# A two-layer decoder trunk on one NeuronCore: the compressed attention branch turned three steps later, one projection step ahead of the first scores, and two start-up jobs on other engines

## The chip, the cores and the metric

The kernel runs on one NeuronCore of a Trainium2 chip, in one launch. Its time is the device time of one execution in microseconds (us). The engines are TensorE (PE in the profile; PEld is its weight load), VectorE (DVE), ScalarE (ACT), GpSimd (POOL) and SyncE (SP), each with its own in-order instruction queue. They wait for each other through semaphores. DMA transfers are issued from an engine's queue and move their data beside it.

## The reference

The trunk has a width of 1024 and 512 positions. Layer 0 mixes with an RG-LRU and a retention head group, layer 1 with a native sparse attention (NSA). Each layer has an FFN behind it. What the change touches is the first projection of layer 0 and the attention of layer 1:

```
def reference(x, ...):
    h = x
    for layer in range(2):
        hn = rmsnorm(h, attn_norm[layer])
        h = h + (hybrid_ab(hn, ...) if layer == 0 else nsa(hn, ...))
        h = h + swiglu(rmsnorm(h, ffn_norm[layer]), ...)
    return rmsnorm(h, final_norm)

def nsa(h, w_in, ..., w_out):              # 16 heads in 4 groups, head size 64
    proj = h @ w_in                        # queries, six K/V sets, gates
    ...
    s = einsum('bqgrd,bngd->bgrqn', qb, kc)         # compressed branch: 31 blocks
    p_cmp = where(vis, softmax(where(vis, s, NEG)), 0)
    o_cmp = einsum('bgrqn,bngd->bqgrd', p_cmp, vc)
    ...                                             # selected and window branches
    o = gb[..., 0:1] * o_cmp + gb[..., 1:2] * o_slc + gb[..., 2:3] * o_win
    return o @ w_out
```

## The kernel before

All products are made in a split form. An operand is kept as a rounded part and a remainder (`whi` and `wlo` for weights, `hgh` and `hgl` for activations, `oh` and `ol` for the attention's output), and three matmuls take the place of one (`mm3`, lines 201 to 203). ACT makes the rounded part by a copy, DVE the remainder by a subtraction. A scheduler takes the program's instructions with priorities and fixes the order on each engine when the kernel is built; at run time every engine then works strictly in that order.

**Start (`layer0`, lines 449 to 478).** PE first runs 20 small matmuls on zeros (`ps_z`, line 373). Then the first projection runs over k = 0..7. Slice k needs a weight slice (`wr`, DMA line 462) and an input slice (`xin`, DMA line 463), 256 KB each, both on SP's queue. ACT rounds the weights (line 464), ACT and DVE make `hgh` (line 234) and `hgl` (line 235) from the input, DVE makes `wlo` (line 466), and PE runs 12 matmuls per k into `ps_x` (lines 476 to 478), in the order of k, since they accumulate.

**Attention (`attention`, from line 1092).** Positions are cut in four tiles of 128, taken in the order 2, 3, 1, 0; a unit is a tile, one of four groups g and its branches. A unit's scores (`head_s`, lines 1174 to 1176), the scaling of its probabilities on POOL (`scale`, line 1194), and their transposes and products with V (lines 1199, 1203, 1206, 1214, 1215) stand three units apart, and the loop runs in slots, four or more to a unit. At a slot's end two things may be advanced by one step:

- `fill`: what is left of layer 1's projection, 20 steps of 6 matmuls (`ps_t`).
- `side`: a list of generators, advanced once a slot (twice if it is longer than 2). One is `compressed(i)` for tile i: scores, maximum, subtraction on POOL, exponential on ACT, sum on DVE, then the multiplication by the gated reciprocal on POOL (line 1136, out and in `pcmp`), some empty steps, four PE transposes (line 1142), the rounded part `pch` on ACT (line 1144) and the remainder `pcl` on DVE (line 1145). Another is `finish`, which carries an output out (`up` line 1226, `o` line 1231, `oh` line 1235, `ol` line 1237).

The last matmuls of an output (`block_v`, lines 1220 and 1221) take `pch` and `pcl` of its tile. The transposes of the compressed branch and those of line 1199 share a pool of two buffers (`ps_tr`), each of which is free when ACT and DVE have read it.

**Output projection (`layer1`).** Behind the last unit, 72 matmuls into `ps_p` (4 output tiles, 6 of 8 slices k, three each) begin before the last outputs are there; slices 0 and 1 come from tile 0's group 0, 2 and 3 from group 1, and so on. Its weights `w1o` are loaded by SP into the buffers (`wr`) that the attention's probabilities use, so that a load waits until a unit's transposes are done, and are then rounded on ACT (line 136) and DVE (line 137).

Of the kernel before, what the change touches and what calls it, by code (L numbers as in the profile page):

```python
# [63 lines left out]
class Trunk:  # L64
# [377 lines left out]
    def layer0(self):  # L442
        nc, a = self.nc, self.a
# [13 lines left out]
        for k in range(KD):  # L457
            x = xin[k // 4][:, k % 4, :]
            c = slice((k % 4) * S, (k % 4 + 1) * S)
            w = raws[k // 4][:, c]  # L460
            hi, lo = (t[:, (k % 2) * S:(k % 2 + 1) * S] for t in wx[k // 2])
            nc.sync.dma_start(w, a["w0t"][k // 4][:, c])
            nc.sync.dma_start(x, a["xT"][k])
            nc.scalar.copy(hi, w)
            self.put_hg(hg, k, x, self.gain[0][:, k:k + 1])
            nc.vector.tensor_tensor(lo, w, hi.bitcast(F32), op=ALU.subtract)
        for k in range(KD):
# [113 lines left out]
        w = [self.unit() for _ in range(4)]  # L581
# [510 lines left out]
    def attention(self, QS, stack, stacked, qlate, halves, KH, KL, VV, kc2, vc, gate, OH, OL, fill):  # L1092


        nc = self.nc
# [4 lines left out]
        def compressed(i):  # L1100

            while not {(i, 0), (i, 1)} <= stacked:
                yield
            q = QS[i]
            pc = self.g2([P, H, 32], name="pcmp")
            pr = pc.rearrange("p (r g) n -> p r g n", g=G)
            mask = self.cmask[:, i:i + 1, :].unsqueeze(1).broadcast_to([P, R, 2, 32])
            for half in range(2):
                ps = self.psA("ps_s")
                ph = ps.rearrange("p (r g z n) -> p r g z n", r=R, g=2, z=2)  # L1110
                for h in range(8 * half, 8 * half + 8):
                    g, r = h // R, h % R
                    T.matmul(ph[:, r, g % 2], q[:, h, :], kc2[:, g], start=True, stop=True)
                    if h % 4 == 3:
                        yield
                dst = pr[:, :, 2 * half:2 * half + 2, :]
                V.tensor_tensor(dst, ph[:, :, :, 0, :], mask, op=ALU.add)
                V.tensor_tensor(dst, ph[:, :, :, 1, :], dst, op=ALU.add)
                yield
            mx = self.s1([P, H], "mx")  # L1120
            V.tensor_reduce(mx, pc, axis=AX.X, op=ALU.max)
            yield
            Q.tensor_tensor(pc, pc, mx.unsqueeze(2).broadcast_to([P, H, 32]), op=ALU.subtract)
            yield
            A.activation(pc, pc, AF.Exp)
            yield
            sc = self.s1([P, H], "sc")
            V.tensor_reduce(sc, pc, axis=AX.X, op=ALU.add)
            V.reciprocal(sc, sc)
            gv = gate[:, i, :].rearrange("p (g r b) -> p b r g", g=G, r=R)  # L1130
            s3 = sc.rearrange("p (r g) -> p r g", r=R)
            V.tensor_tensor(s3, s3, gv[:, 0], op=ALU.mult)
            if i == 0:
                V.tensor_scalar(sc, sc, self.vis0, None, op0=ALU.mult)
            yield
            Q.tensor_tensor(pc, pc, sc.unsqueeze(2).broadcast_to([P, H, 32]), op=ALU.mult)
            yield
            yield
            pt = self.psC("ps_tr")
            pcf = pc.rearrange("p h n -> p (h n)")  # L1140
            for r in range(R):
                T.transpose(pt[:, r * P:(r + 1) * P], pcf[:, r * P:(r + 1) * P], self.ident)
            ch, cl = (self.g2([P, S], F32R, name="pc" + n) for n in "hl")
            A.copy(ch, pt)
            V.tensor_tensor(cl, pt, ch.bitcast(F32), op=ALU.subtract)
            cmp_pt[i] = ch, cl
            yield

        def late(t):
            QS[t] = self.b8([P, H, P], F32R, name="qs")  # L1150
            for c in range(2):
                stack(t, qlate[:, halves[1].index(t), 8 * c:8 * c + 8, :].rearrange("p h d -> p (h d)"), c)
                yield
# [11 lines left out]
        def head_s(u, r):  # L1165
            if r == 0:
                u.p = self.probs().rearrange("p (r b x) -> p r b x", r=R, b=u.n)
                u.rs = self.sm.tile([P, R, u.n], F32, tag="rs", name="rs")
                u.kh, u.kl = (x[u.g // 2][:, u.bs[0]:u.bs[-1] + 1, u.g % 2, 0:u.nk] for x in (KH, KL))
            h = R * u.g + r  # L1170
            ps = self.psA("ps_s")
            u.ps = ps[:, 0:u.n * u.nk].rearrange("p (b x) -> p b x", b=u.n)
            q = QS[u.i][:, h, :]
            T.matmul(u.ps, q, u.kh, start=True, stop=False)
            T.matmul(u.ps, q, u.kl, start=False, stop=False)
            T.matmul(u.ps[:, :, u.i * P:u.nk], self.identr, self.triNeg.unsqueeze(1).broadcast_to([P, u.n, P]), start=False, stop=True)

        def head_m(u, r):
            u.nm = self.sm.tile([P, 2], F32, tag="nm", name="nm")
            V.tensor_reduce(u.nm[:, 0:u.n], u.ps, axis=AX.X, op=ALU.max, negate=True)  # L1180

        def head_e(u, r):
            for b in range(u.n):
                A.activation(u.p[:, r, b, 0:u.nk], u.ps[:, b, :], AF.Exp, bias=u.nm[:, b:b + 1], accum_out=u.rs[:, r, b:b + 1])  # L1184
# [11 lines left out]
        def block_t(u, b, j):  # L1196
            u.pt = self.psC("ps_tr")
            for r in range(R):
                T.transpose(u.pt[:, r * P:(r + 1) * P], u.p[:, r, b, j * P:(j + 1) * P], self.ident)
            u.th, u.tl = (self.g2([P, S], F32R, name="pt" + n) for n in "hl")  # L1200

        def block_hi(u, b, j):
            A.copy(u.th, u.pt)

        def block_lo(u, b, j):
            V.tensor_tensor(u.tl, u.pt, u.th.bitcast(F32), op=ALU.subtract)
            u.last = u.th, u.tl
# [36 lines left out]
        def advance():  # L1244
            if side and next(side[0], 0) == 0:
                side.pop(0)
                advance()
# [4 lines left out]
        for n in range(len(units) + LAG):  # L1252
            us = units[n] if n < len(units) else None
            if n >= len(units):

                self.plan("w1o", n - len(units), 2048)
                self.load()
                self.prefetch(2)
            un = units[n - 1] if 0 <= n - 1 < len(units) else None
            uv = units[n - LAG] if n >= LAG else None  # L1260
            if us is not None and us.g == us.bs[0] == 0:
                at = tiles.index(us.i)
                if at + 1 < NT:
                    t = tiles[at + 1]
                    side += ([late(t)] if t in halves[1] else []) + [compressed(t)]
            nb = len(uv.blocks) if uv else 0
            for sl in range(max(R, nb)):
                hd = us.heads[sl] if us and sl < R else None
                bl = uv.blocks[sl] if sl < nb else None
                while us and (us.i, us.g // 2) not in stacked:  # L1270
                    if next(fill, 0) == 0:
                        advance()
                if hd:
                    head_s(*hd)
                if bl:
                    block_t(*bl)
                if hd:
                    with prio(offset=12):
                        head_m(*hd)
                if bl:  # L1280
                    block_hi(*bl)
                if hd:
                    with prio(offset=-6):
                        head_e(*hd)
                if bl:
                    with prio(offset=-12):
                        block_lo(*bl)
                if un and sl < R:
                    if sl == 0:
                        with prio(offset=-6):  # L1290
                            norm(un)
                    scale(un, sl)
                if len(pend) >= 2:
                    args = pend.pop(0)
                    block_v(*args)
                    u, b, j = args[:3]
                    if u.bs[b] == 1 and j == u.i:
                        side.insert(0, finish(u.i, u.g))
                if bl:
                    pend.append(bl + uv.last)  # L1300
                for _ in range(2 if len(side) > 2 else 1):
                    advance()
                next(fill, 0)
# [138 lines left out]
```

## Time and profile before

| | us |
|---|---|
| median of three runs | 1243.75 |
| lowest and highest of them | 1243.32, 1243.83 |
| the profiled execution, its own time | 1243.25 |
| its span, first to last instruction | 1241.3 |
| PE busy | 1221.3 |
| DVE busy | 797.6 |
| ACT busy | 684.3 |
| POOL busy | 230.8 |

All times of the trace count from the span's first instruction. The start of the kernel is at 0 to 20, the attention with its slots at about 672 to 850, and the output projection and the second FFN follow.

### The profile page before, as it was taken

How to read it: one execution, taken by the hardware profiler on the slowest of the kernel's cores; microseconds unless marked ns; L12 is line 12 of the kernel's file. 1: busy time of each engine (PE TensorE's matmuls, PEld its weight loads, DVE VectorE, ACT ScalarE, POOL GpSimd, SP SyncE). 2: the span in 40 equal slices, each digit the busy share in tenths (PEclk: the TensorE clock that was granted, in tenths of full speed). 3: DMA queues.
4: the chain of work that ended last, by engine and by line, in shares of the span. 5: the costliest groups of instructions: out<-in, count | busy, mean ns of one | idle time of the engine just before them, and what ended most of it. 6: DMA issues, size and time to landing. Idle time of an engine off the chain costs nothing.

```text
span 1241.3 us, 16441 instructions
## 1 busy us (share of the span) xinstructions
PE 1221.3 (98%) x6077; PEld 1030.5 (83%) x6077; DVE 797.6 (64%) x1237; ACT 684.3 (55%) x1395; POOL 230.8 (19%) x303
## 2 busy tenths in 40 slices
PE   9999999999999999999999999999999999999997
PEld 8788888888888889987888878877888888889996
DVE  6886639666356636775264889985976546653664
ACT  6541447664256426655454688995766336633653
POOL 0001420220012002100000567681111011101200
PEclk9999999999999999999999999999999999999999
DMA  9221143784378428852100000124588358825832
GB/s 343 69 102 68 35 169 102 174 187 150 101 182 184 133 69 178 222 201 77 68 35 1 1 1 1 35 96 171 130 182 200 107 124 185 200 81 107 181 90 68
DMA packets 35535, 149.23 MB, mean 120 GB/s; under 512 B 3936, under 2 KB 6256, under 8 KB 26624
## 3 DMA queue, kind: packets, MB, share of 16 engines
q1 hardware_dynamic: 21296, 100.88, 22.7%
q0 software_dynamic: 14016, 47.27, 21.4%
q8 instruction: 48, 0.79, 0.3%
q14 instruction: 31, 0.25, 0.1%
q10 hardware_dynamic: 144, 0.04, 0.0%
HBM read 143.98 MB, written 4.19 MB: 119 GB/s over the span
## 4 chain that ended last, share of the span: by engine, by line
PE 87%; ACT 5%; DVE 4%; issue 1%; POOL 1%; DMA 0%; POOLq 0%; DVEq 0%; SPq 0%; ACTq 0%
PE ps L203 6%; PE ps L201 6%; PE ps L202 6%; PE ps_t L201 5%; PE ps_t L203 5%; PE ps_t L202 5%; PE ps_X L201 5%; PE ps_X L203 5%; PE ps_X L202 5%; PE ps_V L201 3%; PE ps_V L203 3%; PE ps_V L202 3%; ACT prob L1184 2%; PE ps_Y L201 2%; PE ps_Z L201 2%; PE ps_Z L203 2%
## 5 line engine op out<-in xcount | busy, mean ns | idle before, releaser
L136 ACT CAST whi<-wr 128x512 fp32r<-128x512 f32 (+1 forms) x540 | 294.9, 593 | 347.2 <-PE ps L202 126.0
L137 DVE TENSOR_TENSOR wlo<-wr,whi 128x1024 fp32r<-128x1024 f32 (+2 forms) x272 | 313.4, 1154 | 209.1 <-ACT whi L136 201.9
L201 PE MATMUL ps<-gh,whi 128*128 128x512 f32 (+1 forms) x364 | 139.8, 384 | 0.0
L203 PE MATMUL ps<-gh,wlo 128*128 128x512 f32 (+1 forms) x364 | 139.2, 382 | 0.0
L202 PE MATMUL ps<-gl,whi 128*128 128x512 f32 (+1 forms) x364 | 139.1, 382 | 0.0
L161 POOL DMA_DIRECT2D wr<-wff x64 | 55.5, 866 | 376.1 <-DVE wlo L137 329.4
L201 PE MATMUL ps_t<-whi,hgh 128*128 128x512 f32 x288 | 114.7, 399 | 0.0
L202 PE MATMUL ps_t<-wlo,hgh 128*128 128x512 f32 x288 | 113.4, 394 | 0.0
L203 PE MATMUL ps_t<-whi,hgl 128*128 128x512 f32 x288 | 112.7, 391 | 0.0
L201 PE MATMUL ps_X<-whi,sg 128*128 128x512 f32 (+1 forms) x288 | 107.1, 372 | 0.4 <-DVE part L290 0.3
L203 PE MATMUL ps_X<-whi,sg 128*128 128x512 f32 (+1 forms) x288 | 106.9, 371 | 0.0
L202 PE MATMUL ps_X<-wlo,sg 128*128 128x512 f32 (+1 forms) x288 | 106.8, 371 | 0.0
L1194 POOL TENSOR_TENSOR prob<-prob,rs 128x384 f32<-128x384 f32 (+3 forms) x128 | 88.0, 721 | 1.9
L767 DVE TENSOR_TENSOR h<-ps,h 128x512 f32<-128x512 f32 x46 | 31.8, 691 | 82.5 <-PE ps L203 82.5
L203 PEld LDWEIGHTS ps<-gh,wlo 128*128 128x128 f32 x364 | 68.4, 188 | 13.4
L202 PEld LDWEIGHTS ps<-gl,whi 128*128 128x128 f32 x364 | 68.4, 188 | 13.1
L201 PEld LDWEIGHTS ps<-gh,whi 128*128 128x128 f32 x364 | 68.4, 188 | 12.9
L1184 ACT ACTIVATE prob<-ps_s,nm 128x384 f32<-128x384 f32 (+3 forms) x128 | 68.1, 540 | 15.8 <-DVE nm L1180 15.0
L201 PE MATMUL ps_V<-whi,sg 128*128 128x512 f32 (+1 forms) x192 | 71.4, 372 | 0.0
L203 PE MATMUL ps_V<-whi,sg 128*128 128x512 f32 (+1 forms) x192 | 71.2, 371 | 0.0
L202 PE MATMUL ps_V<-wlo,sg 128*128 128x512 f32 (+1 forms) x192 | 71.2, 371 | 0.0
L203 PEld LDWEIGHTS ps_t<-whi,hgl 128*128 128x128 f32 x288 | 54.1, 188 | 11.5 <-issue 0.2
(316 smaller groups left out, 2565.2 us busy)
## 6 DMA issues: line engine op xcount, KB each, us to landing
wr<-wff POOLq DMA_DIRECT2D x64, 512.0 KB, 5.7
wr<-wff SPq DMA_DIRECT2D x24, 1024.0 KB, 4.8
wr<-wfg POOLq DMA_DIRECT2D x32, 384.0 KB, 5.8
wr<-w0t SPq DMA_DIRECT2D x10, 1024.0 KB, 6.0
wr<-w1t SPq DMA_DIRECT2D x10, 1024.0 KB, 4.9
wr<-wfg SPq DMA_DIRECT2D x12, 768.0 KB, 4.4
wr<-w2a SPq DMA_DIRECT2D x8, 1024.0 KB, 4.8
wr<-w2c SPq DMA_DIRECT2D x8, 1024.0 KB, 4.9
```

The source lines that it names most:

```text
L136: self.nc.scalar.copy(hi[:, c], x[:, c])
L137: self.nc.vector.tensor_tensor(lo, x, hi.bitcast(F32), op=ALU.subtract)
L161: self.nc.gpsimd.dma_start(x[:, c], more[:, c], accum_op=ALU.add)
L201: mm(ps, ah, bh, start=(first and k == 0), stop=False)
L202: mm(ps, ah, bl, start=False, stop=False)
L203: mm(ps, al, bh, start=False, stop=(last and k == n - 1))
L767: V.tensor_tensor(hm, ps, hm, op=ALU.add)
L1184: A.activation(u.p[:, r, b, 0:u.nk], u.ps[:, b, :], AF.Exp, bias=u.nm[:, b:b + 1], accum_out=u.rs[:, r, b:b + 1])
L1194: Q.tensor_tensor(x, x, u.rs[:, r, b:b + 1].broadcast_to([P, u.nk]), op=ALU.mult)
```

## The change

Three edits are made together. First, the DMA of the first input slice is issued from ACT's queue in place of SP's, and the first weight slice is rounded by DVE in place of ACT. Second, `compressed` has five empty steps between the multiplication on POOL and the transposes, where it had two. Third, when the attention has run `fill` until the first queries are stacked, it runs `fill` by one step more before the first scores.

```
             nc.sync.dma_start(w, a["w0t"][k // 4][:, c])
-            nc.sync.dma_start(x, a["xT"][k])
-            nc.scalar.copy(hi, w)
+            (nc.sync if k else nc.scalar).dma_start(x, a["xT"][k])
+            if k:
+                nc.scalar.copy(hi, w)
+            else:
+                nc.vector.tensor_copy(hi, w)
             self.put_hg(hg, k, x, self.gain[0][:, k:k + 1])
...
             Q.tensor_tensor(pc, pc, sc.unsqueeze(2).broadcast_to([P, H, 32]), op=ALU.mult)
-            yield
-            yield
+            for _ in range(5):
+                yield
             pt = self.psC("ps_tr")
...
-                while us and (us.i, us.g // 2) not in stacked:
-                    if next(fill, 0) == 0:
-                        advance()
+                if us and (us.i, us.g // 2) not in stacked:
+                    while (us.i, us.g // 2) not in stacked:
+                        if next(fill, 0) == 0:
+                            advance()
+                    next(fill, 0)
```

Lines of the changed kernel are numbered three higher behind the first edit, and five higher behind the third.

The first place is the start of ACT's queue. `DMAHW1` to `DMAHW7` are the semaphores of the transfers; before, 1 is `w` of k = 0, 2 `x` of k = 0, 3 and 4 `w` and `x` of k = 1, 5 and 6 those of k = 2, and 0 the small table `vec`. Before:

```order
L375 ACT_TABLE_LOAD
L375 COPY ones_89<-ones_89 128x4 [waits DVE_49]
L464 CAST whi_115<-wr_113 128x512 [waits DMAHW1_49]
L234 ACTIVATE hgh_107<-xin_111,vec_87 128x512 [waits DMAHW2_49,DMAHW0_49]
L325 ACTIVATE acc_123<-xin_111 128x512
L464 CAST whi_115<-wr_113 128x512 [waits DMAHW3_49]
L234 ACTIVATE hgh_107<-xin_111,vec_87 128x512 [waits DMAHW4_49]
L328 ACTIVATE sq_173<-xin_111 128x512
L464 CAST whi_117<-wr_113 128x512 [waits DMAHW5_49]
```

In the changed kernel semaphores 2 and 3 are `w` and `x` of k = 1, and 4 is `x` of k = 0, the transfer that ACT itself issues:

```order
L375 ACT_TABLE_LOAD
L375 COPY ones_89<-ones_89 128x4 [waits DVE_49]
L463 DMA xin_111<-xT 128x512
L465 CAST whi_115<-wr_113 128x512 [waits DMAHW2_49]
L234 ACTIVATE hgh_107<-xin_111,vec_87 128x512 [waits DMAHW3_49,DMAHW0_49]
L234 ACTIVATE hgh_107<-xin_111,vec_87 128x512 [waits DMAHW4_49]
L465 CAST whi_117<-wr_113 128x512 [waits DMAHW5_49]
```

The weights of k = 0 have left ACT, and `hgh` of k = 0 (the row that waits for `DMAHW4`) now stands behind the weights and behind `hgh` of k = 1.

The second place is ACT's queue at the end of the attention, from the transposed probabilities `pth` of tile 0's group 1 on. `whi` with `wr` are the weights `w1o` of the output projection, in two loads (`DMAHW4`, `DMAHW5`); the first `up` of each piece is that of tile 0's group 0. Before, `pch` of tile 0 (line 1144) stands eleven rows ahead of this piece:

```order
L1203 CAST pth_7670<-ps_tr_7665 128x512 [waits PE_49]
L1226 COPY up_7680<-ps_o_7622 64x512 [waits PE_49,Activation_49]
L1203 CAST pth_7701<-ps_tr_7696 128x512 [waits PE_49,Activation_49]
L136 CAST whi_7641<-wr_7639 128x512 [waits DMAHW4_49]
L136 CAST whi_7646<-wr_7639 128x512 x2
L136 CAST whi_7641<-wr_7639 128x512
L1235 CAST oh_5415<-o_7682 128x2x128 [waits DVE_49]
L1203 CAST pth_7710<-ps_tr_7705 128x512 [waits PE_49,Activation_49]
L136 CAST whi_7799<-wr_7694 128x512 [waits DMAHW5_49]
```

In the changed kernel (`pch` is line 1147, `pth` 1206, `up` 1229):

```order
L1206 CAST pth_7661<-ps_tr_7656 128x512 [waits PE_49]
L136 CAST whi_7632<-wr_7630 128x512 [waits DMAHW4_49]
L136 CAST whi_7637<-wr_7630 128x512
L136 CAST whi_7632<-wr_7630 128x512
L136 CAST whi_7637<-wr_7630 128x512
L1147 CAST pch_7674<-ps_tr_7669 128x512 [waits PE_49]
L136 CAST whi_7799<-wr_7693 128x512 [waits DMAHW5_49]
L136 CAST whi_7804<-wr_7693 128x512
L136 CAST whi_7799<-wr_7693 128x512
L136 CAST whi_7804<-wr_7693 128x512
L1229 COPY up_7680<-ps_o_7613 64x512 [waits PE_49]
L1206 CAST pth_7700<-ps_tr_7695 128x512 [waits Activation_49]
```

`pch` of tile 0 now stands behind the four casts of the first load, and `up` of group 0 and `pth` of group 2 behind the four of the second.

The third place is PE's queue around the first scores, in the changed kernel; `ps_tr` are the transposes that stack the first queries, `ps_t` the step of `fill`, `ps_s` the scores:

```order
L1025 MATMUL ps_tr_5458<-ident_194,qt_5408 128x128 x3
L201 MATMUL ps_t_5474<-whi_5302,hgh_4280 128x512 [waits PE_49]
L202 MATMUL ps_t_5474<-wlo_5303,hgh_4280 128x512
L203 MATMUL ps_t_5474<-whi_5302,hgl_4282 128x512
L201 MATMUL ps_t_5474<-whi_5302,hgh_4280 128x512
L202 MATMUL ps_t_5474<-wlo_5303,hgh_4280 128x512
L203 MATMUL ps_t_5474<-whi_5302,hgl_4282 128x512
L1177 MATMUL ps_s_5483<-kh_4643,qs_5248 128x384 [waits DVE_49]
L1178 MATMUL ps_s_5483<-kl_4645,qs_5248 128x384
L1179 MATMUL ps_s_5483<-triNeg_4544,identr_4542 128x128
```

Before, the three rows of the scores follow the transposes at once, and the six of `ps_t` follow the scores.

## Rows read from the trace of the kernel before

**Rows 1.** The page: each engine's busy time, and the last chain by engine.
```profile
PE 1221.3 (98%) x6077; PEld 1030.5 (83%) x6077; DVE 797.6 (64%) x1237; ACT 684.3 (55%) x1395; POOL 230.8 (19%) x303
...
PE 87%; ACT 5%; DVE 4%; issue 1%; POOL 1%; DMA 0%; POOLq 0%; DVEq 0%; SPq 0%; ACTq 0%
```

**Rows 2.** Windows: us; busy PE, PEld, DVE, ACT, POOL; PE clock, DMA share, GB/s.
```profile
0.00:20.00 20.00, 18.70 (x81) 16.03 (x82) 14.35 (x27) 15.53 (x28) 0.94 (x5) 1.00 0.91 330
...
720.00:740.00 20.00, 17.73 (x109) 14.62 (x108) 17.01 (x36) 15.65 (x40) 13.23 (x19) 1.00 0.01 2
...
860.00:1215.00 355.00, 354.85 (x1692) 304.19 (x1691) 221.86 (x280) 193.62 (x359) 42.60 (x49) 1.00 0.59 141
...
1235.00:1241.00 6.00, 0.00 (x0) 0.00 (x0) 1.91 (x3) 0.00 (x0) 0.00 (x0) 0.52 0.52 175
```

**Rows 3.** PE's waits, the first: what, for what; us in total, times, longest.
```profile
PE ps_tr L1142 <- POOL pcmp L1136: 1.7, 1, 1.7
```

**Rows 4.** Timeline of PE, start: start us, us, instruction [idle before <-releaser].
```profile
1.09 4.63 PE L373 MATMUL ps_z<-z 128*128 128x128 f32 x20 [1.09 <-DVE sp_acc L429]
5.93 0.70 PE L476 MATMUL ps_x<-hgh,whi 128*128 128x512 f32 x1 [0.21 <-ACT hgh L234]
6.47 0.40 PE L477 MATMUL ps_x<-hgh,wlo 128*128 128x512 f32 x1
```

**Rows 5.** Timeline of ACT, start: `hgh` of k=0, weights and `hgh` of k=1.
```profile
5.16 0.72 ACT L234 ACTIVATE hgh<-xin,vec 128x512 fp32r<-128x512 f32 x1
...
6.31 0.60 ACT L464 CAST whi<-wr 128x512 fp32r<-128x512 f32 x1
6.82 0.72 ACT L234 ACTIVATE hgh<-xin,vec 128x512 fp32r<-128x512 f32 x1
```

**Rows 6.** Timeline of DVE, start: the weights' remainder, k=0.
```profile
5.08 0.69 DVE L466 TENSOR_TENSOR wlo<-wr,whi 128x512 fp32r<-128x512 f32 x1 [4.01 <-ACT whi L464]
```

**Rows 7.** Timeline of PE at the first scores.
```profile
674.49 0.44 PE L1174 MATMUL ps_s<-kh,qs 128*128 128x384 f32 x1 [1.15 <-DVE qs L1028]
...
675.75 0.40 PE L201 MATMUL ps_t<-whi,hgh 128*128 128x512 f32 x1
675.98 0.39 PE L202 MATMUL ps_t<-wlo,hgh 128*128 128x512 f32 x1
```

**Rows 8.** Timelines of POOL, DVE, PE where tile 2's compressed branch is turned.
```profile
703.89 1.05 POOL L1136 TENSOR_TENSOR pcmp<-pcmp,sc 128x512 f32<-128x512 f32 x1
...
706.62 1.37 DVE L1206 TENSOR_TENSOR ptl<-ps_tr,pth 128x512 fp32r<-128x512 f32 x2
...
707.45 0.63 PE L1142 MATMUL ps_tr<-ident,pcmp 128*128 128x128 f32 x4 [1.29 <-POOL prob L1194]
```

**Rows 9.** Timelines of POOL and DVE where tile 3's is turned.
```profile
733.15 1.05 POOL L1136 TENSOR_TENSOR pcmp<-pcmp,sc 128x512 f32<-128x512 f32 x1
...
735.01 0.69 DVE L1180 TENSOR_REDUCE nm<-ps_s 128x1 f32<-128x512 f32 x1 [2.14 <-PE ps_s L1176]
```

**Rows 10.** SP's timeline: the loads of `w1o`.
```profile
831.46 10.67 SPq L117 DMA_DIRECT2D wr<-w1o  x4
```

**Rows 11.** Timeline of ACT at the end of the attention.
```profile
830.15 0.64 ACT L1144 CAST pch<-ps_tr 128x512 fp32r<-128x512 f32 x1
...
836.14 0.58 ACT L1203 CAST pth<-ps_tr 128x512 fp32r<-128x512 f32 x1
836.62 2.18 ACT L136 CAST whi<-wr 128x512 fp32r<-128x512 f32 x4
...
839.99 1.66 ACT L136 CAST whi<-wr 128x512 fp32r<-128x512 f32 x3 [0.40 <-DMA wr<-w1o]
```

**Rows 12.** Timeline of PE there: group 0's last matmul, first and 27th of `ps_p`.
```profile
833.88 0.39 PE L1221 MATMUL ps_o<-pcl,vc 128*128 128x512 f32 x1
...
839.16 0.73 PE L201 MATMUL ps_p<-oh,whi 128*128 128x512 f32 x2 [0.45 <-ACT oh L1235]
...
849.25 0.50 PE L202 MATMUL ps_p<-ol,whi 128*128 128x512 f32 x1
```

## The prediction

> **What bounds the kernel now.** I read the page first. PE is busy for 1221.3 of the span of 1241.3 us and carries 87% of the chain that ended last [rows 1], so the time is PE's work plus PE's idle time, some 20 us. No edit adds or removes a matmul: the question is only which idle time of PE goes and which comes. The windows show where it lies and how firmly the rest is tied to it: in 860 to 1215 PE is busy for 354.85 of 355 us [rows 2], so what is lost or won ahead of it goes straight to the end. Then PE's list of waits: two of its longest stand at the compressed branch's transposes (line 1142), 1.7 and 1.3 us [rows 3, 8]. Last the timelines of the four places that the change touches.
>
> The profiled execution took 1243.25 us, 1.95 more than its span, and lies 0.5 under the median. The sum below is made of shifts against that execution, and put on the median. A measurement can tell about 0.2% from no change, which is 2.5 us here.
>
> **Start.** Before, the zeros keep PE until 1.09 + 4.63 = 5.72, and the first product starts at 5.93, 0.21 later and 0.05 behind the end of `hgh` of k = 0 (5.16 + 0.72 = 5.88) [rows 4, 5]. So even an input that came far earlier could give back only 0.21 us. What the order makes of ACT's queue is another thing: `hgh` of k = 0 stands behind `whi` and `hgh` of k = 1 there. When it runs no longer hangs on its own transfer but on the input of k = 1. `hgh` of k = 1 started at 6.82 [rows 5]; with one transfer less ahead of it on SP's queue its input comes earlier by at most one slice, 256 KB at the window's 330 GB/s [rows 2], 0.79 us. It starts between 6.03 and 6.82, then. `hgh` of k = 0 follows 0.63 later (its 0.72 less the overlap of 0.09 that the rows at 6.31 and 6.82 show [rows 5]), takes 0.72, and PE starts 0.05 behind: 7.43 to 8.22. That is 1.5 to 2.3 later than 5.93. Before, the second matmul came 0.54 behind the first where the steady pace is 0.23 [rows 4, 7]; if a start behind a longer idle stretch does without that 0.31, the loss is 1.2. Bounds +1.2 and +2.3; I take **+1.8**, the middle. The rounding on DVE costs nothing: nearest is `wlo` with 0.69 [rows 6]; no row has DVE rounding from fp32, so I bound it by 0 and twice 0.69. At either end `whi` and `wlo` of k = 0 are there by 4.4 + 1.38 + 0.69 = 6.5, before PE can start; the cover is the late `hgh`, and without it 0.6 us would show.
>
> In 0 to 20 the 16 DMA engines are 91% busy [rows 2]. The Trainium skill ("Trainium Kernel Development and Optimization", section Key Constraints) says that DMAs from the queues of SP, ACT and POOL run on the same 16 engines, and that issuing from several engines saves only the issue time. By that rule the input of k = 0 hardly comes earlier and this edit's gain is nothing; by an independent second path it would be the 0.21 of PE's zeros. The trace speaks for the rule; the sum takes neither.
>
> **First scores.** PE waited 1.15 us for `qs` before the scores at 674.49 [rows 7]. Now six matmuls stand there, 6 x 0.23 = 1.38 (the pace from 675.75 to 675.98 [rows 7]): the wait is filled, and that step is missing at the end of `fill`, where the slots then run a step earlier into the stretch in which DVE and POOL set the pace. Bounds: -1.15, if the other engines keep up there, and -0.5, if half comes back as waits. I take **-1.15**: at the end of `fill`, up to the wait at 707.45 [rows 8], the list of PE's waits has none of any length.
>
> **Tile 2's turn.** The profile puts the 1.29 before 707.45 down to POOL's `prob`, but POOL had multiplied `pcmp` by 703.89 + 1.05 = 704.94 [rows 8]. What came last is on DVE: the first of the two `ptl` from 706.62, halfway through 1.37 at 707.31, which frees the `ps_tr` buffer [rows 8]. The next transposes in PE's queue take a buffer of the same pool, so the wait has a new owner and stays. Bounds -1.3 and 0; I take **0**.
>
> **Tile 3's turn.** Here the wait of 1.7 is real: the multiplication ended at 733.15 + 1.05 = 734.20, and DVE stood idle for 2.14 in the same stretch [rows 3, 9]. Three slots more cover it, and POOL still does the multiplication first. The most is DVE's 2.14, the least half of the wait, 0.85, if the buffers of `ps_tr` are late next. I take **-1.7**. Tile 1's turn is not in PE's list of waits.
>
> **Tile 0's turn, the end of the attention.** The three slots cost something here, since nothing follows that could cover them. Before, `pch` ran at 830.15, group 0 ended at 833.88, `ps_p` began at 839.16 and by 849.25 had 26 of its 72 matmuls behind it [rows 11, 12]; the other 46 at 0.229 end near 859.8. Now `pch` stands behind four casts of the first load of `w1o`, and `up` of group 0 and `pth` of group 2 behind the four of the second. The first load was issued at 831.46, and its casts ran at 836.62, right behind a `pth` [rows 10, 11]: it landed at most 5.2 after its issue. It waits for a buffer whose transposes now stand some 1 us further ahead in PE's queue, without the four of line 1142 and three products ahead of them. So: landing 835.6, casts until 837.8 (2.18), `pch` 838.4, the second load's casts from 839.0 (it held ACT up until 839.99 [rows 11], 1 us less) to 841.2, `up` 841.8 and `pth` 842.4 (0.58 each), `ptl` on DVE (0.69, half of 1.37 [rows 8]) 843.1. Eight transposes and four products, 1.7 us, and `ps_p` begins near 844.8, with 72 matmuls (16.5) and six of the attention (1.4) to come: 862.7 against 859.8, rounded to **+3.0**. If the loads land as before, all is 1 us later: +4.0. If both had landed before ACT asks, ACT would run on from `pth` at about 833.9 (2.2 ahead of 836.14, as group 1's work is now ahead [rows 11]): two groups of casts, `pch`, `up`, `pth`, `ptl` end at 840.7, the whole at 860.4: +0.6.
>
> **The sum.** 1.8 - 1.15 + 0 - 1.7 + 3.0 = +1.95, so 1243.75 + 1.95 = 1245.7 us. All low ends give 1.2 - 1.15 - 1.3 - 2.14 + 0.6 = -2.8, or 1241.0; all high ends 2.3 - 0.5 + 0 - 0.85 + 4.0 = +4.95, or 1248.7.
>
> **Rivals.** *The end is hidden.* If the loads of `w1o` land before ACT asks for them, the fourth term is 0.6 in place of 3.0: 1243.3. For it: ACT reached the first casts only at 836.62 before, so the landing is known from above alone [rows 11]. Against it: ACT did wait 0.40 for the second load, though it came to it at 839.6 [rows 11]. It decides at a first landing before 833.9.
>
> *Slower: the clock falls at the start.* PE would sit idle from 5.72 to between 7.4 and 8.2 in place of 0.21 us. At the span's end, with no matmul at work, the window shows a mean granted clock of 0.52 [rows 2], which is the lower level, 1.2 GHz, of the two; at the start the mean is 1.00. If the clock is lost in the gap and takes as long to come back as the zeros ran, 4.63 us [rows 4], half of that is lost: +2.3, 1248.0. Against it: in 720 to 740 PE idled for 2.27 us in all, and the granted clock stayed at 1.00 [rows 2]. It decides at whether the first `ps_x` matmuls are spaced about 0.46 or 0.23. The Trainium skill ("TensorE: Matmul & The Clock Gate", section The HAM clock gate) has PE at 1.2 GHz by default and back there after idling; this trace agrees at its end alone, so the case keeps one chance in eight.
>
> *Tile 2's wait was POOL's after all.* Then -1.3 comes on top: 1244.4. DVE's rows speak against it.
>
> *Faster.* The end hidden and tile 2's wait gone as well, with the start at its low end and tile 3 at its high one: -2.4 - 1.3 - 0.6 - 0.44 on the forecast, 1241.0. One condition carries it: that ACT's queue at the end runs through without a stop, as it would if loads came 3 us earlier.
>
> **How the numbers follow.** The forecast's own case, +0.2 to +3.6 (1243.9 to 1247.4), has 0.50; of it 0.17 lie over 0.2%. The end hidden 0.20, tile 2 0.08 (both within 0.2%), the clock 0.12 (slower), faster 0.10. So faster 0.10, same 0.33 + 0.20 + 0.08 = 0.61, slower 0.29. The range goes from 1241.5 to 1248.5, which leaves out most of the faster case and the upper ends of the clock's.
>
> **What would show it.** Start: `hgh` of k = 0 behind that of k = 1 on ACT, and the first `ps_x` at 7.4 to 8.2; at 5.9 the term is gone. First scores: no wait of 1.15 before `ps_s`, six `ps_t` ahead. Tile 3: no wait at line 1145 (1142 before); tile 2: a wait of about 1.3 for `ptl`, at line 1202 or 1145. End: ACT idle before the first `whi` of `w1o`, `pch` at about 838, PE waiting several us in all between 834 and 845. The forecast is wrong above all if ACT doesn't idle there, or if PE's clock is low behind the start.

## The result, and the profile after

The changed kernel takes 1253.69 us (median of six runs, 1252.45 to 1254.91) against 1244.01 before (six runs, 1243.32 to 1246.02). The ratio is 1.0075, with a 95% interval from 1.0062 to 1.0088: 9.7 us slower, outside the range given, and on the slower side. The profiled execution took 1253.94, its span is 1251.9, 10.6 more than before. Times in this document are medians, while a ratio and its interval weigh every run, so that the two can differ by 1 us (experiment 8: 5.5 us by the medians, 6.5 by the ratio). Two executions, one of experiment 5 and one of experiment 11, ran at a lower granted clock throughout (mean 0.85 and 0.65) and count in no time below, but the trace of experiment 5 is of the first of them.

The windows of the changed kernel (us; busy PE, PEld, DVE, ACT, POOL; granted PE clock, DMA share, GB/s) have in their clock column what no row of before had ahead of the end:

```profile
0.00:20.00 20.00, 16.09 (x61) 13.59 (x61) 13.96 (x27) 14.88 (x28) 0.94 (x5) 1.00 0.92 329
...
720.00:740.00 20.00, 19.38 (x126) 17.08 (x125) 19.00 (x42) 16.88 (x44) 14.25 (x21) 1.00 0.01 2
740.00:760.00 20.00, 19.12 (x115) 15.13 (x115) 18.46 (x35) 17.67 (x42) 13.49 (x16) 1.00 0.00 1
760.00:780.00 20.00, 19.05 (x118) 16.34 (x119) 18.81 (x37) 16.99 (x41) 16.13 (x20) 1.00 0.00 1
780.00:800.00 20.00, 19.52 (x119) 15.85 (x117) 18.02 (x31) 18.64 (x51) 13.41 (x19) 1.00 0.16 54
...
840.00:860.00 20.00, 17.36 (x66) 13.75 (x65) 12.35 (x17) 9.86 (x20) 5.00 (x10) 0.76 0.62 236
```

From 840 to 860 the mean granted clock is 0.76: PE was at the lower of its two levels (1.2 in place of 2.4 GHz) for about half of that stretch. 0 to 20 reads 1.00 and still had a slow stretch, as PE's timeline of the start shows by the pace; it answers to [rows 4]:

```profile
1.09 4.63 PE L373 MATMUL ps_z<-z 128*128 128x128 f32 x20 [1.09 <-DVE sp_acc L429]
8.55 0.80 PE L479 MATMUL ps_x<-hgh,whi 128*128 128x512 f32 x1 [2.82 <-ACT hgh L234]
9.14 0.63 PE L480 MATMUL ps_x<-hgh,wlo 128*128 128x512 f32 x1
9.57 0.63 PE L479 MATMUL ps_x<-hgh,whi 128*128 128x512 f32 x1
...
13.39 0.40 PE L481 MATMUL ps_x<-hgl,whi 128*128 128x512 f32 x1
13.63 0.40 PE L479 MATMUL ps_x<-hgh,whi 128*128 128x512 f32 x1
```

PE waits 2.82 us for `hgh`, and the first products follow each other 0.43 apart; only from 13.39 on it is 0.23. The first product is 2.6 later than before, the transposes ahead of the first scores 4.6 (676.93 against 672.31). The records of the granted clock begin at its first change, here the rise near 13.4, and the time ahead of them counts as 1.00 in the window; so the column of the first window can't be trusted, but the pace can. The zeros take 4.63 us in both kernels, and in runs in which the clock rose during them they take less (4.11 and 3.83 in the traces of experiments 1 and 4). So in this execution the clock did not fall in the gap: it had not risen yet and stayed low until 13.4, where before it was up from the second product on.

ACT's timeline of the start (against [rows 5]) has the weights of k = 1 at 6.01 and then both `hgh` in one group, that of k = 1 ahead:

```profile
6.01 0.62 ACT L465 CAST whi<-wr 128x512 fp32r<-128x512 f32 x1 [3.34 <-DMA wr<-w0t]
7.16 1.33 ACT L234 ACTIVATE hgh<-xin,vec 128x512 fp32r<-128x512 f32 x2 [0.53 <-DMA xin<-xT]
```

At the first scores the wait of 1.15 is gone ([rows 7]); PE's list of waits (what, for what; us in total, times, longest) no longer has the POOL row of [rows 3], but it has new or longer ones, from the start (the first), from the attention and from its end:

```profile
PE ps_x L479 <- ACT hgh L234: 2.8, 1, 2.8
PE ps_tr L1202 <- DVE ptl L1209: 2.7, 6, 0.9
PE ps_o L1217 <- ACT pth L1206: 1.9, 2, 1.5
PE ps_o L1224 <- DVE pcl L1148: 1.7, 1, 1.7
```

PE's timeline there, against [rows 12]:

```profile
834.07 0.40 PE L1224 MATMUL ps_o<-pcl,vc 128*128 128x512 f32 x1
...
838.69 0.50 PE L1217 MATMUL ps_o<-pth,vv 128*128 128x512 f32 x1 [1.46 <-ACT pth L1206]
839.51 1.09 PE L1145 MATMUL ps_tr<-ident,pcmp 128*128 128x128 f32 x4 [0.32 <-DVE ptl L1209]
...
844.93 0.50 PE L1224 MATMUL ps_o<-pcl,vc 128*128 128x512 f32 x1 [1.65 <-DVE pcl L1148]
...
847.08 0.76 PE L1217 MATMUL ps_o<-pth,vv 128*128 128x512 f32 x1 [0.98 <-DVE o L1234]
...
851.72 0.63 PE L201 MATMUL ps_p<-oh,whi 128*128 128x512 f32 x1
```

The row at 834.07 is the last product of tile 1; in the kernel before it stands at 830.35. So tile 1 ends 3.7 late, `ps_p` begins 12.6 late (851.72 against 839.16), and products that take 0.39 at the upper level of the clock take 0.63. ACT and DVE there, against [rows 11]:

```profile
838.99 2.20 ACT L136 CAST whi<-wr 128x512 fp32r<-128x512 f32 x4
841.07 0.61 ACT L1147 CAST pch<-ps_tr 128x512 fp32r<-128x512 f32 x1
842.80 2.18 ACT L136 CAST whi<-wr 128x512 fp32r<-128x512 f32 x4 [1.12 <-DMA wr<-w1o]
...
840.71 3.57 DVE L137 TENSOR_TENSOR wlo<-wr,whi 128x1024 fp32r<-128x1024 f32 x2 [0.75 <-ACT whi L136]
844.20 0.68 DVE L1148 TENSOR_TENSOR pcl<-ps_tr,pch 128x512 fp32r<-128x512 f32 x1
```

`pcl`, which one product of every group of tile 0 needs, stands behind 3.57 us of DVE's work on the weights of the output projection.

### The profile page after: what moved, and what is told of

It is laid out like the page before. It is cut to its first block, busy times and chain, and to the rows that moved or that the text cites. A ratio compares the mean times of both kernels' runs of the same rounds, so it can differ in the third digit from the quotient of the medians.

```text
span 1251.9 us, 16442 instructions
## 1 busy us (share of the span) xinstructions
PE 1227.5 (98%) x6077; PEld 1036.3 (83%) x6077; DVE 798.2 (64%) x1238; ACT 684.3 (55%) x1394; POOL 231.0 (18%) x303
## 4 chain that ended last, share of the span: by engine, by line
PE 84%; DVE 6%; ACT 5%; DMA 1%; issue 1%; POOL 1%; POOLq 0%; SPq 0%; DVEq 0%; ACTq 0%
PE ps L201 6%; PE ps L203 6%; PE ps L202 6%; PE ps_t L201 5%; PE ps_t L203 5%; PE ps_t L202 5%; PE ps_X L201 4%; PE ps_X L203 4%; PE ps_X L202 4%; PE ps_V L201 3%; PE ps_V L203 3%; PE ps_V L202 3%; PE ps_Z L203 2%; PE ps_Z L201 2%; PE ps_Z L202 2%; PE ps_Y L201 2%
```

## The experiments

Each was timed beside the kernel before, on the same chip; "before" is its time there. The theory was that all of the loss comes from two places where PE idles, is late and runs at the lower level of its clock; the rivals stand in the expectations.

**1. The start alone** (1248.49 us, before 1244.41; ratio 1.0033, 1.0020 to 1.0045).

```
+            (nc.sync if k else nc.scalar).dma_start(x, a["xT"][k])
+            if k: nc.scalar.copy(hi, w)
+            else: nc.vector.tensor_copy(hi, w)
```

> Only the first edit: the first input slice on ScalarE's queue and the first weight slice rounded by VectorE. Theory (late hgh of k = 0 plus a fall of PE's clock): the first ps_x product at about 8.5 us in place of 5.93, products 0.43 apart until about 13.4, and the whole 4.7 us slower than before, all of it kept to the end. Rival (part of the start's loss is absorbed further on): the same start, but 2.5 to 3 us slower in all.

4.1 us slower, and the first product at 8.41 in its trace, with the slow pace until 11.3 (the expectation: 13.4). The interval, 2.5 to 5.6 us, does not exclude the rival's 3; the trace does for its own execution. PE is 4.8 late at the transposes ahead of the first scores (677.06 against 672.31), 4.8 at the last product of tile 1 (835.14 against 830.35) and 4.8 at the last `ps_p` (891.59 against 886.82): what is lost at the start stays lost.

**2. The start, with PE kept at work** (1246.49, before 1244.41; ratio 1.0015, 1.0006 to 1.0024).

```
-        for i in range(10):    # 20 matmuls on zeros
+        for i in range(18):    # 36
```

> The first edit, with 36 matmuls on zeros ahead of the first product in place of 20, so that PE is at work until about 7.5 us. Theory (it was PE's idle stretch of 2.8 us that cost the clock): the products run 0.23 apart from the start, and the whole is 2.6 us slower than before, 2.0 less than with the first edit alone. Rival (the clock falls for another reason, or the zeros' extra time only delays the products): as slow as the first edit alone, 4.7 us over before, or more.

```profile
1.09 7.06 PE L373 MATMUL ps_z<-z 128*128 128x128 f32 x36 [1.09 <-DVE sp_acc L429]
8.44 0.50 PE L479 MATMUL ps_x<-hgh,whi 128*128 128x512 f32 x1 [0.28 <-ACT hgh L234]
...
9.85 0.39 PE L480 MATMUL ps_x<-hgh,wlo 128*128 128x512 f32 x1
10.08 0.40 PE L481 MATMUL ps_x<-hgl,whi 128*128 128x512 f32 x1
```

PE's timeline: the first product comes as late as in experiment 1, but behind 0.28 of idle time; no product takes 0.63, and from 9.61 on the pace is 0.23 to 0.24. By the times, 2.0 us of experiment 1's 4.1 are the clock, 2.1 the delay.

**3. Only the rounding on DVE** (1244.27, before 1244.41; ratio 0.9999, 0.9990 to 1.0008).

```
             nc.sync.dma_start(x, a["xT"][k])
+            if k: nc.scalar.copy(hi, w)
+            else: nc.vector.tensor_copy(hi, w)
```

> Of the first edit only the rounding of the first weight slice on VectorE; the input slice stays on SP's queue. Theory (it is the DMA's move that puts hgh of k = 0 behind that of k = 1): the first product at 5.9, no change, within 0.5 us of before. Rival (the rounding's move alone changes ScalarE's order): 2 us or more slower.

No change, as the theory had it. In its trace the first product stands at 6.25, 0.3 later than before; in that of experiment 6, whose start is the old one, it stands at 6.30, so this is not the rounding's doing.

**4. Only the DMA's move** (1248.77, before 1244.41; ratio 1.0033, 1.0022 to 1.0045).

```
+            (nc.sync if k else nc.scalar).dma_start(x, a["xT"][k])
             nc.scalar.copy(hi, w)
```

> Of the first edit only the DMA's move: the first input slice on ScalarE's queue, rounding on ScalarE as before. Theory (the DMA's move alone is the loss): the first product at 7.5 to 8.6 us and the clock low for some 5 us, 3.5 to 4.7 us slower than before. Rival (the loss needs both moves, since with the rounding ahead of it ScalarE reaches hgh of k = 0 in the old order): the product at 6.3 to 7, 0.5 to 1.5 us slower.

```profile
6.16 0.62 ACT L464 CAST whi<-wr 128x512 fp32r<-128x512 f32 x1 [0.91 <-DMA wr<-w0t]
7.16 1.33 ACT L234 ACTIVATE hgh<-xin,vec 128x512 fp32r<-128x512 f32 x2 [0.38 <-DMA xin<-xT]
```

The same order and the same 7.16 on ACT, and the whole loss, 4.4 us: it is the DMA's move. This trace also shows a fall of the clock in the gap. PE's timeline, and two windows as above:

```profile
1.09 3.83 PE L373 MATMUL ps_z<-z 128*128 128x128 f32 x20 [1.09 <-DVE sp_acc L429]
8.55 0.79 PE L476 MATMUL ps_x<-hgh,whi 128*128 128x512 f32 x1 [3.63 <-ACT hgh L234]
```

```profile
3.90:7.30 3.40, 1.02 (x9) 0.83 (x8) 1.18 (x2) 1.37 (x3) 0.00 (x0) 1.00 0.96 357
7.30:14.10 6.80, 5.55 (x13) 4.40 (x14) 6.29 (x11) 6.80 (x13) 0.00 (x0) 0.50 1.05 389
```

The clock was up while the last zeros ran, and down from 7.3 on, 2.4 us after PE had gone idle.

**5. The first slice issued first on ACT's queue** (1246.46, before 1244.69; ratio 1.0012, 1.0003 to 1.0021).

```
+        nc.scalar.dma_start(xin[0][:, 0, :], a["xT"][0])   # ahead of the table's DMA
         self.setup()
```

> The first edit, with the first input slice issued as the first thing on ScalarE's queue, ahead of the small table: hgh of k = 0 then stands ahead of the weights and hgh of k = 1 there. Theory (what costs is that hgh of k = 0 waits behind k = 1's transfers, and the clock falls in that idle stretch): the first product at 6.2 to 6.7 us, no fall of the clock behind it, within 0.8 us of before. Rival (a second queue makes the first transfers themselves late, whatever the order): the first product past 7 us, 2 us or more slower than before.

```profile
5.29 0.63 ACT L325 ACTIVATE acc<-xin 128x512 f32<-128x512 f32 x1 [2.15 <-DMA xin<-xT]
6.48 0.72 ACT L234 ACTIVATE hgh<-xin,vec 128x512 fp32r<-128x512 f32 x1 [0.56 <-DMA vec<-vec]
```

Neither came out as told; both have a part. With `hgh` of k = 0 ahead in the queue it starts at 6.48, not behind the one that starts at 7.16, and over half of the loss is gone (1.8 us left in place of 4.1). But the slice, issued first of all, is there only at 5.29 (before, `hgh` ran at 5.16 with the slice second on SP's queue), and the table, now second on ACT's queue, holds ACT up until 6.48. The first product comes at 7.26, past the rival's 7, and the products run 0.43 apart from 8.7 to 11.7, which the theory had ruled out. Neither order tried on ACT's queue beats SP's.

**6. The projection step alone** (1244.90, before 1244.52; ratio 1.0004, 0.9995 to 1.0013).

```
+                    next(fill, 0)      # behind the loop that waits for `stacked`
```

> Only the third edit: one projection step of six matmuls ahead of the first scores. Theory (the wait of 1.15 us is filled and stays filled): 1.0 to 1.2 us faster than before. Rival (the step is missed at the end of the projection, where VectorE sets the pace, and the gain is given back): within 0.4 us of before.

The rival: no gain can be measured. In its trace the wait of 1.15 is gone, but from 700 to 820 us PE is busy for 113.47 where it was 115.08 before, 1.6 less: the gain went back in that stretch. The list of waits still has tile 3's 1.7 and tile 2's (1.3 before), now put down to DVE, and new small ones, the longest for DVE:

```profile
PE ps_tr L1142 <- POOL pcmp L1136: 1.7, 1, 1.7
...
PE ps_tr L1142 <- DVE ptl L1206: 1.0, 1, 1.0
...
PE ps_tr L1199 <- DVE rs L1188: 0.6, 1, 0.6
```

**7. The five steps alone** (1251.88, before 1244.52; ratio 1.0069, 1.0057 to 1.0082).

```
-            yield
-            yield
+            for _ in range(5):
+                yield
```

> Only the second edit: five empty steps in place of two ahead of the compressed branch's transposes, for all four tiles. Theory (tile 0's turn comes late, PE idles, its clock falls there, and that outweighs the wait saved at tile 3): 4 to 5 us slower than before, with a stretch at half clock between 835 and 855. Rival (the late turn costs its delay alone, 3 us, less the 1.7 of tile 3): 1 to 1.5 us slower, no stretch at half clock.

7.4 slower, more than expected, and with the low clock that the theory named (840 to 860 reads 0.83). The scheduler's order differs here from that with the extra step. In its trace PE also waits within the attention (for `pth`, 4.0 us in four waits, the longest 2.7), and at the end once for long, behind the casts of `w1o` on ACT:

```profile
847.64 0.77 PE L1214 MATMUL ps_o<-pth,vv 128*128 128x512 f32 x1 [4.15 <-ACT whi L136]
```

**8. The five steps and the projection step** (1250.01, before 1244.52; ratio 1.0052, 1.0040 to 1.0065).

> The second and the third edit without the first. Theory (the edits add up): the changed kernel's time less the 4.7 us of its start, 5 us slower than before. Rival (the start's delay had moved the end's loads and so made the late turn dearer): 3 us slower or less.

5.5 slower. With the 4.1 of the start that is 9.6, and the changed kernel has 9.7: the edits add up, within the noise of about 1 us of each.

**9. The projection step, and five steps for tiles 2 and 3 alone** (1244.79, before 1244.52; ratio 1.0008, 0.9999 to 1.0017).

```
-            for _ in range(5):
+            for _ in range(5 if i >= 2 else 2):
```

> The third edit, and the second for tiles 2 and 3 alone; tiles 1 and 0 keep two empty steps. Theory (the whole loss of the attention is tile 0's late turn): no stretch at half clock, the waits at tile 3 and at the first scores gone, 1 to 2.5 us faster than before. Rival (the waits come back elsewhere in the attention, as in the changed kernel, where by the end of tile 1 only 1 us was won): within 0.7 us of before; if slower by 2 us, tile 0 isn't the cause.

The loss is gone, so it is tile 0's (or tile 1's) turn; but no gain appears, though both waits are gone from its list. The theory's gain is wrong, its place of the loss is right. A second sign of the theory failed as well, for its trace has a low stretch:

```profile
840.00:860.00 20.00, 19.18 (x77) 14.97 (x78) 9.46 (x13) 6.42 (x13) 3.67 (x4) 0.91 0.54 193
```

It comes behind two waits of 0.72 and 0.81 among the first `ps_p`, hardly longer than the 0.45 and 0.80 that the kernel before has there without a fall. Five of its eleven runs, the profiled one among them, took 1246.2 to 1248.2, the other six 1244.2 to 1244.8; even these are not measurably faster than the 1244.52 before.

**10. The projection step, and five steps for tile 0 alone** (1249.92, before 1244.69; ratio 1.0043, 1.0029 to 1.0057).

```
+            for _ in range(5 if i == 0 else 2):
```

> The third edit, and the second for tile 0 alone; the other tiles keep two empty steps. Theory (tile 0's late turn makes the loss): as slow as the second and third edit together or slower by the wait at tile 3, 1250 to 1252, with a stretch at half clock near 840 to 853. Rival (the loss comes from the other tiles' changed order): within 1 us of before.

5.2 slower, and 840 to 860 reads 0.83: tile 0's turn it is.

**11. Extra matmuls at the end, first try** (1250.03, before 1244.69; ratio 1.0041, 1.0026 to 1.0055). Experiment 8 and, in `block_v` for groups 0 to 2 of tile 0:

```
+                    for _ in range(6):
+                        T.matmul(ps[:, 0:P], self.ident, self.ident, start=True, stop=True)
```

> The second and the third edit, with 18 matmuls on the identity, whose output nobody reads, put among the last products of tile 0, where PE waits for ScalarE and VectorE. Theory (some 4 of the 7 us that the end of the attention loses are PE's half clock, and the clock falls because PE idles there): no half clock there, 2.5 to 4 us faster than the same kernel without them, 1246 to 1247.5. Rival (the waits alone set the end, or the clock falls all the same): 1250, or later by what of the 18 (0.2 each) is not hidden.

Not told apart by the time. Nothing holds these matmuls back, so they ran from 831 to 839.6, and the waits for `pcl` (1.41) and the next `pth` (1.13) stayed behind them. The clock held where they ran (820 to 840 reads 1.00, in experiment 8 0.91) and fell behind the two waits:

```profile
840.00:860.00 20.00, 17.86 (x70) 14.33 (x71) 9.27 (x16) 6.54 (x14) 2.94 (x4) 0.83 0.57 211
```

**12. Extra matmuls where PE waits** (1246.90, before 1244.17; ratio 1.0017, 1.0007 to 1.0026). Experiment 8 and three groups of six; each takes an operand of tile 0 (`tl`, `ch`, `cl`), so that it runs behind that operand.

```
+                    for _ in range(6):
+                        T.matmul(ps, self.identr, ch, start=True, stop=True)
```

> The second and the third edit, with three groups of six matmuls whose output nobody reads. Each takes pth, pch or pcl of tile 0 as an operand, so that it runs where PE waited longest at the end of the attention: ahead of group 1's first pth (1.5 us), between pch and pcl (1.7) and behind pcl (1.0). In the run before this one the extra matmuls ran too early and the two last waits stayed. Theory (PE's idling makes the clock fall there): no half clock between 830 and 855, and 2 to 3.5 us faster than the second and third edit alone, 1246.5 to 1248. Rival (the clock falls for another reason, or PE's waits shift as much as is filled): a stretch at half clock as before, 1250 to 1251.5.

The windows of experiment 8, and then of this one:

```profile
820.00:840.00 20.00, 15.97 (x90) 12.31 (x89) 16.85 (x35) 18.73 (x63) 13.20 (x34) 0.91 0.32 107
840.00:860.00 20.00, 19.03 (x82) 15.50 (x82) 7.92 (x14) 6.00 (x12) 2.93 (x4) 0.91 0.56 211
```

```profile
820.00:840.00 20.00, 18.29 (x108) 14.38 (x107) 16.52 (x34) 18.75 (x65) 14.18 (x36) 1.00 0.31 107
840.00:860.00 20.00, 19.24 (x89) 15.76 (x90) 8.70 (x16) 6.82 (x14) 2.95 (x4) 1.00 0.59 211
```

The clock stays at 1.00, and although PE has 18 products of 0.23 more to do, the kernel is 3.1 us faster than experiment 8 (1246.90 against 1250.01; 2.8 when each is taken against its own before). The theory holds: PE's idling there makes the clock fall. How much of the 3.1 is the clock is less sure. In the two traces the stretch from tile 1's last product to the last `ps_p` is only 1.2 shorter than in experiment 8 (60.5 against 61.7), extra products included, and experiment 8's trace has a wait of 1.3 in the second FFN (line 201, for line 286 on ACT) that this one has not. In the changed kernel's trace the same stretch takes 63.0. So the clock at the end costs 1.2 to 3.1. The 2.7 that are left against before are the delay of tile 0's turn less what the attention kept.

No version beats the kernel before by more than can be measured.

## Why the prediction was wrong

**The clock.** This is the step that failed: the sum has PE's clock at nothing, at the start and at the end. At the start it stood among the rivals: "Slower: the clock falls at the start" was priced well (+2.3; experiment 2 measures 2.0), but given one chance in eight. At the end the prediction forecast "PE waiting several us in all" and drew nothing from it for the clock: 1.2 to 3.1 us missing from the sum (experiment 12). The reason against it was that 2.27 us of idle time in 720 to 740 had left the clock at 1.00 [rows 2]. That stretch is two waits of PE before:

```profile
730.38 0.63 PE L1199 MATMUL ps_tr<-ident,prob 128*128 128x128 f32 x4 [0.53 <-DVE ptl L1206]
...
734.25 0.66 PE L1142 MATMUL ps_tr<-ident,pcmp 128*128 128x128 f32 x4 [1.74 <-POOL pcmp L1136]
```

At the end of the changed kernel the waits are 1.46, 0.32, 1.65 and 0.98 within 10 us; the longest is shorter than the 1.74, but there are 4.4 us of them. One stretch that kept its clock could not carry the conclusion for two others. The Trainium skill ("TensorE: Matmul & The Clock Gate", section The HAM clock gate) has PE return to 1.2 GHz after idling; experiment 4 agrees, with the clock down from 7.3 on in a gap of 3.63 us. The prediction had named the two signs of its being wrong, and both came: PE's clock was low behind the start, and ACT did not idle ahead of the first load's casts.

**Start, +1.8.** The mechanism was right, `hgh` of k = 0 behind that of k = 1, and experiments 3 and 4 show that the DMA's move alone makes it. The size of the delay measures 2.1 (experiment 2), inside the bounds; in the trace the first product is even later than the upper bound, 8.55 against 8.22. What the bound missed: it let the input of k = 1 come earlier by a place in the queue, and it came later (7.16 against 6.82). From 4.5 to 5.5 us ACT's queue moved 0.19 MB and SP's 0.13, where SP's had moved 0.32 before: the slice on ACT's queue took from those on SP's. From 3 to 4 us all queues together moved only 195 GB/s, against 304 before; why is not shown. The Trainium skill ("Trainium Kernel Development and Optimization", section Key Constraints) says they interleave and only issue time is saved; experiment 5's 5.29 for a slice issued first agrees. The rounding cost nothing, as forecast (experiment 3). The lower bound rested on the 0.54 between the first two products before; by the pace of the changed kernel that is the low level of the clock, not the price of a start.

**First scores, -1.15.** The wait was filled, as forecast: the first scores run at 679.18, 4.7 late with six products more behind them, where the start alone had made PE 4.6 late. But in all nothing came of it (experiment 6). The failed half is "at the end of `fill` ... the list of PE's waits has none of any length": that list is of the kernel before, and in experiment 6 PE has 1.6 more of idle time from 700 on, where `fill` has ended. That it is the missing step which opens these waits is likely, not shown.

**Tile 2 and 3, 0 and -1.7.** Tile 2's wait changed its owner and stayed, as forecast: 0.94 for `ptl`, now ahead of line 1202. Tile 3's is gone in place: window 720 to 740 has PE busy for 19.38 in place of 17.73. What failed is the assumption that a wait removed there stays removed. The three windows behind it had 19.72, 19.61 and 19.80 of PE before:

```profile
740.00:760.00 20.00, 19.72 (x121) 16.18 (x120) 19.61 (x38) 17.48 (x42) 14.55 (x19) 1.00 0.01 1
760.00:780.00 20.00, 19.61 (x121) 16.34 (x120) 18.28 (x34) 17.92 (x42) 16.81 (x20) 1.00 0.00 1
780.00:800.00 20.00, 19.80 (x122) 16.39 (x121) 18.63 (x35) 18.74 (x60) 11.43 (x19) 1.00 0.16 54
```

and have 19.12, 19.05 and 19.52 after, 1.4 less. In both kernels DVE and ACT are busy for 17 to 19.6 us of each 20 there. From 700 to 820 as a whole PE is busy for 115.08 before and 115.00 after: its idle time was moved, not removed. PE came earlier into a stretch that other engines pace, and waited. By the end of tile 1 the lateness is 3.7 where the start made 4.6: of a forecast 2.85, 0.9 is left. Experiment 9 agrees: both waits gone, no gain, though in its trace a low stretch of 3.4 us hides up to half of that.

**End, +3.0.** The delay was right in kind, its size at the upper bound, 4.0: in experiment 12, where the clock holds, tile 1 ends 0.5 earlier than before (829.87 against 830.35) and the last `ps_p` 3.6 later (890.39 against 886.82), 4.1 in between, some of which may be the extra products. By the times 2.7 are left of it in all. Two links of the chain were other than told. The first load was no stop: ACT came to its casts at 838.99 without a wait, since ACT itself was late; it did wait 1.12 for the second load. And the wait for `pcl` came from DVE, where two `wlo` of 3.57 together stood ahead of it.

**The sum, with the sizes measured.** In the two profiled executions: the first product 2.6 late, 2.0 more by the low clock behind it, 0.9 kept in the attention, the end 6.5 (of which 4.1 stand in experiment 12 as well, where the clock holds, so that some 2.4 are the clock), and 0.3 behind it: 10.5, against 10.6 in the spans. By the times: 4.1 (experiment 1) and 5.5 (experiment 8), 9.6 against 9.7.

## What to carry to other kernels

Where a sum makes the busiest engine wait, price the wait twice: once for its length, and once for what the granted clock does behind it, by the pace of the products in the rows. Before counting a removed wait as gain, look at the engines in the stretch behind it: here two others are busy for nine tenths, and the wait came back in small pieces. And a step put off by a few slots cost nothing that could be measured in the middle of the pipeline (experiment 9), but at its end it fell behind the next stage's preparation in the in-order queues of ACT and DVE.

## What the runs showed of the hardware

The length of an idle gap alone does not tell at which level of the clock the products behind it start. In the trace of experiment 6 PE idled for 1.17 us ahead of the first product and the products ran at the upper level; in that of experiment 3 it idled for 0.52 and they ran at the lower one until about 10.3:

```profile
6.30 0.51 PE L476 MATMUL ps_x<-hgh,whi 128*128 128x512 f32 x1 [1.17 <-ACT hgh L234]
6.64 0.40 PE L477 MATMUL ps_x<-hgh,wlo 128*128 128x512 f32 x1
```

```profile
6.25 0.79 PE L479 MATMUL ps_x<-hgh,whi 128*128 128x512 f32 x1 [0.52 <-ACT hgh L234]
6.84 0.63 PE L480 MATMUL ps_x<-hgh,wlo 128*128 128x512 f32 x1
```

In experiment 6's trace the zeros had gone through in 4.04 us, in experiment 3's in 4.63, so the clock had risen during them in the one and had yet to rise in the other. Nor does the length of short waits decide a fall: 0.72 and 0.81 us were followed by one in the trace of experiment 9, 0.45 and 0.80 at the same place were not in the kernel before, and 1.74 was not in its 720 to 740. By its times experiment 3 is no slower than the kernel before, so a single execution can lose some 2 us (half of 6.25 to 10.3) at the start by the level of the clock alone. The profiled executions of experiments 6 and 3 took 1243.67 and 1246.50; how much of the scatter between runs of one kernel (the one before: 1243.0 to 1247.5 in these runs) is this was not tried apart.
